# Twenty-four steps of the second block's conditioning moved from the second feed-forward into the first

## The chip, the cores and the metric

The kernel runs on one core of a Trainium2 chip, in one launch. The metric is the device time of one execution in microseconds (us), as the median of three runs.

## The reference, cut to what matters

512 tokens of width 1024 go through two blocks in float32. The first block has three sublayers, each of the form `x + w * gate * norm(fn(norm(x) * (1 + scale) + shift))`: a feed-forward, a mixer and a second feed-forward. The second block has two layers, each a mixer and a mixture of experts. Shift, scale and gate of every sublayer come from a conditioning vector, by one product of a vector with a matrix per block (and per layer in the second block):

```python
def swiglu(h, w_in, w_out):
    g, u = jnp.split(h @ w_in, 2, axis=-1)          # 1024 -> 2 x 2816
    return (jax.nn.silu(g) * u) @ w_out             # 2816 -> 1024
...
ada = (jax.nn.silu(c) @ w_ada[l] + b_ada[l]).reshape(B, N_SUB, 3, D)
...
x = sublayer(x, 0, lambda h: swiglu(h, ffn1_w_in[l], ffn1_w_out[l]), 0.5)
x = sublayer(x, 1, mixer, 1.0)
x = sublayer(x, 2, lambda h: swiglu(h, ffn2_w_in[l], ffn2_w_out[l]), 0.5)
...
def adaln(cond, mod_w, mod_b):                      # second block
    m = jax.nn.silu(cond) @ mod_w + mod_b           # 1024 -> 6 x 1024
    return jnp.split(m, 6, axis=-1)
...
sh1, sc1, g1, sh2, sc2, g2 = [m[:, None, :] for m in adaln(c, mod_w[i], mod_b[i])]
if need_ctx_in:                                     # layer 0 alone
    csh1, csc1, cg1, csh2, csc2, cg2 = adaln(c_ctx, mod_w[i], mod_b[i])
```

The conditioning of the second block depends on nothing that the first block computes, so it may be done at any time before the second block begins.

## The kernel before, in words

**Layout and products.** Activations lie transposed: 1024 channels in eight groups of 128 partitions, 512 tokens along the free side. Every float32 weight chunk (mostly 128 x 1024, 512 KB) is loaded by SyncE into a `raw` buffer (four of them), cast by ScalarE to a high half (L159) and reduced by VectorE to a low half (L160). The halves are called `w` (eleven buffers) or `wk` (in one of 25 general tiles, `k4`). A product is three matmuls: high weight by high activation (L164), high by low (L165), low by high (L166). The split activations are `hh` and `hl`. There are three `aux` buffers (tag `mv`), two psum buffers `pb` (gate and up), three `pa` (outputs) and one `pt` (the norms' sums).

**Conditioning.** `mv_group` (L221) cuts a vector-matrix product into steps. A step loads one 512 KB row block of the matrix into an `aux` buffer (L231) and multiplies it by the vector, held ready in a tile, and sums along the row in one VectorE instruction (L235, a multiply-sum). A row that is needed with two vectors (`s2` from `c`, `s3` from `c_ctx`) gets two multiply-sums, the first with its product in a throw-away `junk` tile. The steps wait in a list, `bgq`; `bg(n)` hands out the next n of them at the place in the program where it is called, `bg_flush` all that are left.

**A feed-forward** (`ffn`, L333) has 22 columns of 128 hidden channels in four parts of 7, 6, 6 and 3. Parts one to three work on all 512 tokens: for each column the gate and up weights are loaded, 48 matmuls go to one `pb`, and then `bg(bg)` hands out steps; for each of eight outputs the down weights are loaded, `bg(bg//3)` hands out steps, and the sums are added to `y` (L440). `bg` is 4 in the first feed-forward and 5 in the second. The fourth part flushes the list, loads three pairs of weights and the down weights (`ka`: high half in `k4`, low half in `aux`), and then goes by halves of 256 tokens: gates of three columns, eight outputs, and a boundary. The boundary is the norm of `y`, the addition to x, the norm of x, and the split into the next stage's `hh` and `hl`: its sums over partitions are matmuls of `pt` (L270), its root is taken at L261 and refined at L262 to L264, and the products, residual steps and scalings are L312, L314 and L300. The first half's boundary is thus meant to run beside the second half's matmuls.

**Order.** Each engine works in order. The order is not that of the text alone: a tile scheduler places each instruction by its priority, which follows the text (pieces in `with self.soon()` are moved ahead), as its operands and buffers come free in a simulated time.

**Around the change.** The list in the first feed-forward holds 56 steps of `w_ada` with the small vector steps behind them, and `pre_mixer1` (rope tables and two small vectors). In the second it holds the Silu of `s2` and `s3`, 96 steps of `mod_w` (16 of them with two vectors), vector steps, and the constants of the mixture of experts. The first feed-forward runs from the start to about 404 us, the mixer from there to 665, the second feed-forward to about 1000.

Of the kernel before, what the change touches and what calls it, by code (L numbers as in the profile page):

```python
# [8 lines left out]
F32 = mybir.dt.float32  # L9
# [4 lines left out]
AF = mybir.ActivationFunctionType  # L14
OP = mybir.AluOpType
# [45 lines left out]
class Prog:  # L61
# [161 lines left out]
    def mv_group(self, arr, g, outs, now=False):  # L223

        def step(m):
            def go():
                if now:
                    w = self.k4(F32, "mv")
                else:
                    w = self.aux()  # L230
                self.nc.sync.dma_start(w, arr[g * 8 + m])  # L231
                for i, (s, dst) in enumerate(outs):
                    last = i == len(outs) - 1
                    junk = w if last else self.k4(F32, "junk")
                    self.nc.vector.scalar_tensor_tensor(  # L235
                        junk, w, 1.0, s, op0=OP.mult, op1=OP.mult, accum_out=dst[:, m:m + 1])
            return go
        for m in range(8):
            if now:
                step(m)()  # L240
            else:
                self.bgq.append(step(m))
# [1329 lines left out]
def program(tc, A, stop=None):  # L1572
    nc = tc.nc
    with ExitStack() as ctx:
        K = Prog(tc, A, ctx)
# [30 lines left out]
        with K.soon():  # L1606
# [8 lines left out]
            r, t = (K.pg() for _ in range(2))  # L1615
# [29 lines left out]
        def post_boundary(j, nxt):  # L1645
            def go(hs, acc, y):
                acc2 = K.postnorm(hs, acc, y, Gp1[j])
                if nxt is not None:
                    nxt(hs, acc2)
            return go  # L1650

        ffw = lambda n: (A[n + "_in"], [A[f"{n}_out{i}"] for i in range(len(FF_PARTS))])
# [6 lines left out]
            K.diff_lambda()  # L1659

        K.queue(pre_mixer1)
        K.ffn(h, *ffw("ffn1"), post_boundary(0, to if stop != "ffn1" else None), bg=4, lead=lead)
        K.bg_flush()
        if stop == "ffn1":
# [11 lines left out]
        to2 = To(G1[2], sh1[2])  # L1676
# [7 lines left out]
        if stop == "mix1":  # L1684
            return finish()


        s2, s3 = K.k4(F32, "s2"), K.k4(F32, "s3")
        for t, i in ((s2, 1), (s3, 2)):
            nc.sync.dma_start(t, A["c_rep"][i])  # L1690

        def silus():
            with tc.issue_after(K.gated):
                for t in (s2, s3):
                    nc.scalar.activation(t, t, AF.Silu)

        K.queue(silus)
        mod = [[K.gvec("mod") for _ in range(6)] for _ in range(2)]
        G2 = [[K.gvec("G2") for _ in range(2)] for _ in range(2)]
        cmod = [K.gvec("cm") for _ in range(2)]  # L1700
        Gc = K.gvec("Gc")

        def mod_vecs(l, i):

            for g in range(3 * i, 3 * i + 3):
                nc.vector.tensor_add(mod[l][g], mod[l][g], K.vec("mod_b", 48 * l + 8 * g, 8))
            gn = K.vec(("n1g", "n2g")[i], 8 * l, 8)
            nc.vector.scalar_tensor_tensor(G2[l][i], mod[l][3 * i + 1], 1.0, gn, op0=OP.add, op1=OP.mult)

        def ctx_vecs():  # L1710
            for g in range(2):
                nc.vector.tensor_add(cmod[g], cmod[g], K.vec("mod_b", 8 * g, 8))
            nc.vector.scalar_tensor_tensor(Gc, cmod[1], 1.0, K.vec("n1g", 0, 8), op0=OP.add, op1=OP.mult)

        for l in range(2):
            for g in range(6):
                outs = [(s2, mod[l][g])]
                if l == 0 and g < 2:
                    outs = [(s3, cmod[g])] + outs
                K.mv_group(A["mod_w"][l], g, outs)  # L1720
                if g == 2 and l == 0:
                    K.queue(ctx_vecs)
                if g % 3 == 2:
                    K.queue(lambda l=l, i=g // 3: mod_vecs(l, i))
        if stop == "ffn2":
            K.bgq = []
            to3 = None
        else:
            to3 = To(G2[0][0], mod[0][0], to2.h)
        K.queue(K.moe_consts)  # L1730
        for l in range(2 if stop != "ffn2" else 0):
            K.queue(lambda l=l: K.moe_shift(l, mod[l][3], mod[l][5]))
        K.ffn(to2.h, *ffw("ffn2"), post_boundary(2, to3), bg=5)
        K.bg_flush()
        if stop == "ffn2":
            return finish()
# [2 lines left out]
        for l in range(2):  # L1739
# [10 lines left out]
            def evac2(m, hs, py, acc):  # L1750
# [5 lines left out]
                nc.vector.scalar_tensor_tensor(xm, py, g1[:, m:m + 1], xm, op0=OP.mult, op1=OP.add)  # L1756
                nc.scalar.activation(open_["xg"][m][:, hs], xm, AF.Copy, scale=G2[l][1][:, m:m + 1])
                K.sq_add(xm, acc, m)
# [40 lines left out]
            routed = K.route(open_["lg"])  # L1799
            to_next = To(G2[1][0], mod[1][0]) if l == 0 and stop != "moe0" else None  # L1800
            open_next = K.moe(l, first, routed, tab, g2, to_next, K.odd_first if to_next else None)
# [176 lines left out]
```

## Time and profile before

| | |
|---|---|
| median of the runs | 1971.92 us (1971.67 to 1973.52, 3 runs) |
| profiled execution | 1968.39 us, span 1966.5 us |
| mean granted clock | 0.971 |
| TensorE busy | 1826.9 us, 93% |
| VectorE busy | 1300.0 us, 66% |
| ScalarE busy | 900.6 us, 46% |
| GpSimd busy | 164.4 us, 8% |

Every duration below is from the one profiled execution. PE is TensorE's matmuls, PEld its weight loads, DVE VectorE, ACT ScalarE, POOL GpSimd, SPq the DMA issues of SyncE. PEclk is the granted clock as a share of full speed, the DMA share the mean busy share of 16 DMA engines. A row of a timeline gives the start, the duration, the instruction and, in brackets, how long the engine was idle before it and what ended that. In a row of windows, (x74) counts the instructions of the engine. Matmuls overlap, so the step from one start to the next says more than a matmul's own duration.

### The profile page before, as it was taken

To read this page: it belongs to the slowest core of one execution; us is meant where nothing else is said; L and a number is where in the kernel's file an instruction comes from. 1 tells how busy PE (TensorE), PEld (TensorE's weight loads), DVE (VectorE), ACT (ScalarE), POOL (GpSimd) and SP (SyncE) were. 2 spreads that over 40 slices of the span, in tenths; PEclk is the share of its full clock that TensorE was granted. 3 is DMA by queue.
4 is the path that set the end of the run, shared out by engine and by line. 5 is a ranking of instruction groups with operands and counts; after the bars stand their busy time and mean duration, and the time that the engine had idled before them with its cause. 6 is when DMAs were issued, how large, how long until landed. Compare 5 with 4: busy or idle time off the path is not lost. (4 is left out here: it accounts for less than half of the span.)

```text
span 1966.5 us, 25708 instructions
## 1 busy us (share of the span) xinstructions
PE 1826.9 (93%) x9669; PEld 1502.5 (76%) x9669; DVE 1300.0 (66%) x2205; ACT 900.6 (46%) x1444; POOL 164.4 (8%) x133
## 2 busy tenths in 40 slices
PE   4999999999987999999999998979999799979996
PEld 3778888986746988868898878967666688967663
DVE  8877434686866689888548776656554654457773
ACT  4422323455657552222336664526665632345551
POOL 0000000000000000000000000004442000014431
PEclk9999999999988999999999999989999899979998
DMA  8888333241113247999533000548997523469993
GB/s 325 300 304 287 105 104 98 86 140 64 60 48 118 76 147 258 319 333 317 204 119 126 20 1 1 193 135 269 305 317 265 186 81 128 172 210 350 342 355 82
DMA packets 109474, 361.30 MB, mean 184 GB/s; under 512 B 19593, under 2 KB 20257, under 8 KB 109345
## 3 DMA queue, kind: packets, MB, share of 16 engines
q1 hardware_dynamic: 92640, 328.09, 47.1%
q0 software_dynamic: 16128, 29.41, 5.7%
q10 hardware_dynamic: 576, 2.10, 0.3%
q8 instruction: 79, 1.29, 0.3%
q14 instruction: 51, 0.41, 0.1%
HBM read 354.25 MB, written 34.62 MB: 198 GB/s over the span
## 5 line engine op out<-in xcount | busy, mean ns | idle before, releaser
L160 DVE TENSOR_TENSOR w<-raw,w 128x1024 fp32r<-128x1024 f32 (+3 forms) x192 | 221.8, 1161 | 168.7 <-issue 74.2
L159 ACT CAST w<-raw 128x1024 fp32r<-128x1024 f32 (+3 forms) x192 | 191.2, 1000 | 298.7 <-PE pa L166 95.8
L164 PE MATMUL pb<-hh,w 128*128 128x512 f32 (+1 forms) x800 | 289.3, 364 | 17.6 <-ACT hh L159 14.3
L165 PE MATMUL pb<-hl,w 128*128 128x512 f32 (+1 forms) x800 | 290.1, 363 | 4.7 <-DVE hl L160 4.7
L166 PE MATMUL pb<-hh,w 128*128 128x512 f32 (+1 forms) x800 | 290.4, 363 | 2.0 <-DVE w L160 1.8
L164 PEld LDWEIGHTS pb<-hh,w 128*128 128x128 f32 x800 | 152.2, 191 | 43.5 <-ACT hh L159 16.0
L165 PEld LDWEIGHTS pb<-hl,w 128*128 128x128 f32 x800 | 152.4, 191 | 29.4 <-DVE hl L160 6.7
L166 PEld LDWEIGHTS pb<-hh,w 128*128 128x128 f32 x800 | 152.4, 191 | 26.5 <-DVE w L160 4.1
L160 DVE TENSOR_TENSOR k<-raw,k 128x1024 fp32r<-128x1024 f32 x101 | 121.6, 1219 | 67.2 <-ACT k L159 57.6
L164 PE MATMUL pa<-hh,w 128*128 128x512 f32 (+1 forms) x392 | 142.5, 367 | 3.3 <-ACT sq L286 2.0
L1477 PE MATMUL pb<-w,a 128*128 128x512 f32 x304 | 137.0, 593 | 2.0 <-ACT a L1466 2.0
L165 PE MATMUL pa<-hl,w 128*128 128x512 f32 (+1 forms) x392 | 135.4, 347 | 0.0
L166 PE MATMUL pa<-hh,w 128*128 128x512 f32 (+1 forms) x392 | 135.1, 346 | 0.0
L164 PE MATMUL pa<-k,w 128*128 128x512 f32 x304 | 126.3, 415 | 0.0
L235 DVE SCALAR_TENSOR_TENSOR aux<-aux,s 128x1024 f32<-128x1024 f32 x96 | 115.7, 1221 | 12.1 <-DMA aux<-in_mod_w 11.5
L165 PE MATMUL pa<-act,w 128*128 128x512 f32 x304 | 118.7, 390 | 2.2 <-DVE act L160 2.1
L166 PE MATMUL pa<-k,w 128*128 128x512 f32 x304 | 119.7, 394 | 0.0
L166 PE MATMUL pa<-act,w 128*128 128x512 f32 x304 | 118.4, 390 | 0.9 <-DVE w L160 0.9
L165 PE MATMUL pa<-k,w 128*128 128x512 f32 x304 | 119.2, 392 | 0.0
L164 PE MATMUL pa<-act,w 128*128 128x512 f32 x304 | 118.4, 390 | 0.3 <-ACT w L159 0.3
L159 ACT CAST k<-raw 128x1024 fp32r<-128x1024 f32 x101 | 105.2, 1048 | 8.8 <-DMA tab<-ht 2.6
L1477 PEld LDWEIGHTS pb<-w,a 128*128 128x128 f32 x304 | 57.2, 189 | 60.4 <-issue 53.2
(445 smaller groups left out, 3962.9 us busy)
## 6 DMA issues: line engine op xcount, KB each, us to landing
aux<-in_mod_w SPq DMA_DIRECT2D x96, 512.0 KB
raw<-in_ffn_in SPq DMA_DIRECT2D x88, 512.0 KB
raw<-in_moe_w SPq DMA_DIRECT2D x86, 512.0 KB
aux<-in_w_ada SPq DMA_DIRECT2D x64, 512.0 KB
w<-in_moe_w SPq DMA_DIRECT2D x64, 512.0 KB
k<-in_moe_w SPq DMA_DIRECT2D x42, 512.0 KB
raw<-in_ffn_out SPq DMA_DIRECT2D x32, 384.0 KB
raw<-in_mix_in SPq DMA_DIRECT2D x20, 512.0 KB
```

The lines of the kernel that those rows point to most:

```text
L159: self.cast = self.nc.scalar.copy(hi, src).ins
L160: return self.nc.vector.tensor_sub(lo, src, hi.bitcast(F32)).ins
L164: mm(p, wh, xh, start=start, stop=False)
L165: mm(p, wh, xl, start=False, stop=False)
L166: mm(p, wl, xh, start=False, stop=stop)
L235: self.nc.vector.scalar_tensor_tensor(junk, w, 1.0, s, op0=OP.mult, op1=OP.mult, accum_out=dst[:, m:m + 1])
L1477: nc.tensor.matmul(py[:, ns], a[:, cs], wt[c][:, ns], start=c == 0, stop=c == 1)
```

## The change

In the first feed-forward the list now begins with a piece that loads `c` and `c_ctx` of the second block into `s2` and `s3` and takes their Silu. Behind `pre_mixer1` it ends with three of the twelve groups of the second block's conditioning: groups 0 to 2 of layer 0, 24 steps, 16 of them with two vectors, 40 multiply-sums in all, and the vector steps that go with them. The second feed-forward's list loads `s2` again and takes its Silu again; it has the other 72 steps, and `bg` there is 3 instead of 5. Since the vectors exist only when their piece has run, `mv_group` now looks them up by name. Line numbers behind L233 are higher by one in the changed kernel.

```diff
@@ mv_group
                 for i, (s, dst) in enumerate(outs):
+                    s = self.cvec[s] if isinstance(s, str) else s
                     last = i == len(outs) - 1
@@ before the first feed-forward
         K.queue(pre_mixer1)
+        cvec = {}
+        def silus(*which):
+            def go():
+                for n, i in which:
+                    cvec[n] = K.k4(F32, n)
+                    nc.sync.dma_start(cvec[n], A["c_rep"][i])
+                with tc.issue_after(K.gated):
+                    for n, _ in which:
+                        nc.scalar.activation(cvec[n], cvec[n], AF.Silu)
+            return go
...
+        def mod_group(l, g):
+            outs = [("s2", mod[l][g])]
+            if l == 0 and g < 2:
+                outs = [("s3", cmod[g])] + outs
+            K.mv_group(A["mod_w"][l], g, outs)
+            if g == 2 and l == 0:
+                K.queue(ctx_vecs)
+            if g % 3 == 2:
+                K.queue(lambda: mod_vecs(l, g // 3))
+        K.cvec = cvec
+        K.bgq.insert(0, silus(("s2", 1), ("s3", 2)))
+        for g in range(3):
+            mod_group(0, g)
         K.ffn(h, *ffw("ffn1"), post_boundary(0, to if stop != "ffn1" else None), bg=4, lead=lead)
@@ before the second feed-forward
-        s2, s3 = K.k4(F32, "s2"), K.k4(F32, "s3")
-        for t, i in ((s2, 1), (s3, 2)):
-            nc.sync.dma_start(t, A["c_rep"][i])
...
-        K.queue(silus)
...
+        K.queue(silus(("s2", 1)))
         for l in range(2):
             for g in range(6):
...
+                if l or g > 2:
+                    mod_group(l, g)
...
-        K.ffn(to2.h, *ffw("ffn2"), post_boundary(2, to3), bg=5)
+        K.ffn(to2.h, *ffw("ffn2"), post_boundary(2, to3), bg=3)
```

The order moves in the first feed-forward's last part. The number in a tile's name counts tiles in the order of their allocation, so it is higher in the change: the third column's psum there is `pb_443` before and `pb_504` now.

**TensorE, from the second to the third column of the last part, first half of the tokens, before:**

```order
L165 MATMUL pb_441_2546<-hl_34_123,w_419_2454 128x256
L166 MATMUL pb_441_2546<-hh_33_122,w_420_2455 128x256
L164 MATMUL pb_443_2600<-hh_27_116,w_422_2460 128x256
L165 MATMUL pb_443_2600<-hl_28_117,w_422_2460 128x256
L166 MATMUL pb_443_2600<-hh_27_116,w_423_2461 128x256
```

and now:

```order
L165 MATMUL pb_502_2682<-hl_34_123,w_480_2590 128x256
L166 MATMUL pb_502_2682<-hh_33_122,w_481_2591 128x256
L164 MATMUL pb_504_2736<-hh_27_116,w_483_2596 128x256
L165 MATMUL pb_504_2736<-hl_28_117,w_483_2596 128x256
L164 MATMUL pb_552_3004<-hh_27_116,w_471_2572 128x256
L165 MATMUL pb_552_3004<-hl_28_117,w_471_2572 128x256
L166 MATMUL pb_552_3004<-hh_27_116,w_472_2573 128x256
```

Two matmuls into the third column, TensorE now goes to `pb_552`, the first column of the second half of the tokens, whose 48 matmuls stand before the rest of the third column.

**VectorE, low halves of the last part's weights, before** (`w_420` and `w_423` are low halves of the second and third column, `wk` and `aux` those of the third column's up weights and the down weights):

```order
L160 TENSOR_TENSOR wk_426_2467<-raw_424_2465,wk_425_2466 128x1024
L160 TENSOR_TENSOR w_420_2455<-raw_418_2453,w_419_2454 128x1024
L440 TENSOR_TENSOR pg_143_771<-pg_143_771,pa_404_2389 128x512
L160 TENSOR_TENSOR aux_432_2476<-raw_430_2474,wk_431_2475 128x1024
L160 TENSOR_TENSOR aux_435_2482<-raw_433_2480,wk_434_2481 128x1024
L440 TENSOR_TENSOR pg_143_771<-pg_143_771,pa_408_2415 128x512
L160 TENSOR_TENSOR w_423_2461<-raw_421_2459,w_422_2460 128x1024
L160 TENSOR_TENSOR aux_438_2488<-raw_436_2486,wk_437_2487 128x1024
```

and now (`w_484` is the third column's low half, `wk_487` that of its up weights):

```order
L236 SCALAR_TENSOR_TENSOR junk_440_2387,cm_67_185<-aux_439_2385,s3_131_620 128x1024
L236 SCALAR_TENSOR_TENSOR aux_445_2416,mod_52_170<-aux_445_2416,s2_130_618 128x1024
L236 SCALAR_TENSOR_TENSOR aux_439_2385,mod_51_169<-aux_439_2385,s2_130_618 128x1024
L236 SCALAR_TENSOR_TENSOR aux_450_2445,mod_52_170<-aux_450_2445,s2_130_618 128x1024
L1690 TENSOR_TENSOR cm_67_185<-cm_67_185,c_7_93 128x8
L1684 TENSOR_TENSOR mod_51_169<-mod_51_169,c_7_93 128x8
L160 TENSOR_TENSOR w_484_2597<-raw_482_2595,w_483_2596 128x1024
L236 SCALAR_TENSOR_TENSOR aux_455_2474,mod_52_170<-aux_455_2474,s2_130_618 128x1024
L1691 SCALAR_TENSOR_TENSOR Gc_68_186<-cm_67_185,c_7_93 128x8
L1686 SCALAR_TENSOR_TENSOR G2_62_180<-mod_51_169,c_7_93 128x8
L160 TENSOR_TENSOR wk_487_2603<-raw_485_2601,wk_486_2602 128x1024
L236 SCALAR_TENSOR_TENSOR aux_460_2503,mod_52_170<-aux_460_2503,s2_130_618 128x1024
```

Where low halves followed each other, multiply-sums of the conditioning (L236, `mod` and `cm`) now stand between them.

**TensorE, end of the first feed-forward and start of the mixer, before** (`pa_511` is the last output, `pa_565` and `pb_567` are the mixer's first products):

```order
L164 MATMUL pa_511_3127<-act_429_2473,wk_437_2487 128x256
L165 MATMUL pa_511_3127<-act_429_2473,wk_437_2487 128x256
L166 MATMUL pa_511_3127<-act_429_2473,aux_438_2488 128x256
L164 MATMUL pa_565_3290<-hh_27_116,w_542_3243 128x256
L164 MATMUL pb_567_3342<-w_548_3255,hh_27_116 128x512
L165 MATMUL pb_567_3342<-w_549_3256,hh_27_116 128x512
```

and now (`pa_572` is the last output, `pa_626` and `pb_628` the mixer's first products):

```order
L164 MATMUL pa_572_3263<-act_490_2609,wk_498_2623 128x256
L165 MATMUL pa_572_3263<-act_490_2609,wk_498_2623 128x256
L166 MATMUL pa_572_3263<-act_490_2609,aux_499_2624 128x256
L270 MATMUL pt_541_2956<-acc_525_2909,c_5_89 128x256
L270 MATMUL pt_574_3277<-acc_558_3166,c_5_89 128x256
L164 MATMUL pa_626_3426<-hh_27_116,w_603_3379 128x256
L164 MATMUL pb_628_3478<-w_609_3391,hh_27_116 128x512
L165 MATMUL pb_628_3478<-w_610_3392,hh_27_116 128x512
```

`pt_541` is the first half's second norm, of x; its counterpart before stood 59 matmuls ahead of the last output's end, and now it stands behind it, together with the second half's first norm, `pt_574`.

## Rows read from the trace of the kernel before

**Rows 1.** The forty slices of the page: TensorE's busy tenths and the DMA digits.

```profile
...
PE   4999999999987999999999998979999799979996
...
DMA  8888333241113247999533000548997523469993
...
```

**Rows 2.** Second feed-forward: us; busy PE, PEld, DVE, ACT, POOL; PEclk, DMA, GB/s.

```profile
840.00:860.00 20.00, 17.71 (x74) 13.42 (x74) 17.22 (x27) 5.26 (x7) 0.00 (x0) 1.00 0.89 311
860.00:880.00 20.00, 17.90 (x72) 12.79 (x72) 18.57 (x31) 5.47 (x8) 0.00 (x0) 1.00 0.93 330
```

**Rows 3.** Waits of TensorE, 640 to 1010 us: total us, times, longest us.

```profile
...
PE pb L166 <- DVE w L160: 1.8, 4, 0.5
PE pb L164 <- ACT w L159: 1.3, 2, 1.1
...
```

**Rows 4.** Timeline of TensorE, last part's start and mixer's start: start us, us, instruction.

```profile
...
349.85 0.28 PE L164 MATMUL pb<-hh,w 128*128 128x256 f32 x1
349.97 0.28 PE L165 MATMUL pb<-hl,w 128*128 128x256 f32 x1
...
403.58 0.39 PE L164 MATMUL pa<-hh,w 128*128 128x256 f32 x1 [0.15 <-ACT hh L159]
```

**Rows 5.** Windows of 50 us in the first feed-forward, columns as in rows 2.

```profile
100.00:150.00 50.00, 47.92 (x212) 39.36 (x211) 36.86 (x60) 14.60 (x21) 0.00 (x0) 1.00 0.86 305
300.00:350.00 50.00, 50.00 (x223) 41.43 (x222) 21.29 (x27) 17.93 (x22) 0.00 (x0) 1.00 0.37 115
```

**Rows 6.** Timelines of SyncE's queue (issues) and of ScalarE, 345 to 353 us.

```profile
345.22 0.33 SPq L149 DMA_DIRECT2D raw<-in_ffn_out  x1
...
347.00 0.33 SPq L149 DMA_DIRECT2D raw<-in_ffn_out  x1
...
349.76 1.05 ACT L159 CAST wk<-raw 128x1024 fp32r<-128x1024 f32 x1 [1.79 <-DMA raw<-in_ffn_out]
351.70 1.06 ACT L159 CAST wk<-raw 128x1024 fp32r<-128x1024 f32 x1 [0.89 <-DMA raw<-in_ffn_out]
```

**Rows 7.** Timeline of VectorE in the second feed-forward, two multiply-sums end to end.

```profile
717.20 1.22 DVE L235 SCALAR_TENSOR_TENSOR aux<-aux,s 128x1024 f32<-128x1024 f32 x1
...
718.35 1.22 DVE L235 SCALAR_TENSOR_TENSOR junk<-aux,s 128x1024 f32<-128x1024 f32 x1
```

**Rows 8.** Timeline of VectorE before the last part of the first feed-forward.

```profile
345.75 1.23 DVE L160 TENSOR_TENSOR w<-raw,w 128x1024 fp32r<-128x1024 f32 x1 [0.56 <-PE pa L165]
346.89 0.68 DVE L440 TENSOR_TENSOR pg<-pg,pa 128x512 f32<-128x512 f32 x1
```

**Rows 9.** Timelines of ScalarE and VectorE: the norms' steps, 377 to 404 us.

```profile
377.11 0.42 ACT L286 ACTIVATE sq<-pg 128x256 f32<-128x256 f32 x1 [0.88 <-DVE pg L395]
377.55 1.28 ACT L261 ACT_TABLE_LOAD   x1
378.84 0.47 ACT L261 ACTIVATE hf<-pt,c 128x256 f32<-128x256 f32 x1
...
381.32 0.42 DVE L263 SCALAR_TENSOR_TENSOR hf<-hf,hf 128x256 f32<-128x256 f32 x1
...
382.24 0.76 DVE L312 TENSOR_TENSOR hf<-pg,hf 128x256 f32<-128x256 f32 x2
382.92 0.88 DVE L314 SCALAR_TENSOR_TENSOR x<-hf,ad,x 128x256 f32<-128x256 f32 x2
...
402.16 1.08 ACT L300 ACTIVATE hf<-hf,ad,ad 128x256 f32<-128x256 f32 x2
403.14 0.70 ACT L159 CAST hh<-hf 128x256 fp32r<-128x256 f32 x2
```

**Rows 10.** Windows of 5 us, TensorE alone: us, PE busy, PEclk, DMA share, GB/s.

```profile
660.00:665.00 5.00, 3.00 (x26) 0.99 0.10 7
665.00:670.00 5.00, 5.00 (x29) 0.66 0.83 291
610.00:615.00 5.00, 4.15 (x24) 0.63 0.49 111
```

More of the change, by code (lines that the diff above doesn't have):

```diff
@@ L1661, in program, with mod_vecs, ctx_vecs @@
         K.queue(pre_mixer1)
+        cvec = {}
[8 more added lines that the diff above has]
+            return go
+        mod = [[K.gvec("mod") for _ in range(6)] for _ in range(2)]
+        G2 = [[K.gvec("G2") for _ in range(2)] for _ in range(2)]
+        cmod = [K.gvec("cm") for _ in range(2)]
+        Gc = K.gvec("Gc")
+        def mod_vecs(l, i):
+            for g in range(3 * i, 3 * i + 3):
+                nc.vector.tensor_add(mod[l][g], mod[l][g], K.vec("mod_b", 48 * l + 8 * g, 8))
+            gn = K.vec(("n1g", "n2g")[i], 8 * l, 8)
+            nc.vector.scalar_tensor_tensor(G2[l][i], mod[l][3 * i + 1], 1.0, gn, op0=OP.add, op1=OP.mult)
+        def ctx_vecs():
+            for g in range(2):
+                nc.vector.tensor_add(cmod[g], cmod[g], K.vec("mod_b", 8 * g, 8))
+            nc.vector.scalar_tensor_tensor(Gc, cmod[1], 1.0, K.vec("n1g", 0, 8), op0=OP.add, op1=OP.mult)
+        def mod_group(l, g):
[11 more added lines that the diff above has]
+            mod_group(0, g)
         K.ffn(h, *ffw("ffn1"), post_boundary(0, to if stop != "ffn1" else None), bg=4, lead=lead)
@@ L1685, in program @@
             return finish()
-        s2, s3 = K.k4(F32, "s2"), K.k4(F32, "s3")
-        for t, i in ((s2, 1), (s3, 2)):
-            nc.sync.dma_start(t, A["c_rep"][i])
[L1692 to L1695, printed above, removed]
-        K.queue(silus)
[L1698 to L1713, printed above, removed]
+        K.queue(silus(("s2", 1)))
         for l in range(2):
             for g in range(6):
[L1717 to L1724, printed above, removed]
+                if l or g > 2:
+                    mod_group(l, g)
         if stop == "ffn2":
```

## The prediction

> **What bounds the kernel now.** Three views were read in this order: the forty slices, the windows of the two feed-forwards, and the timelines around the end of the first one. The slices [rows 1] show TensorE at nine tenths or more in most of the first seven and from the fifteenth to the twenty-second; the DMA digits are 8 early in the first feed-forward, then 2 to 3, and up to 9 in the second. So the loads that the change moves leave a stretch with full DMA engines for one with idle ones. The 20 us windows [rows 2] show all that there is to win: TensorE is idle 2.29 and 2.10 us in the two worst windows of the second feed-forward, at a DMA share of 0.89 and 0.93, and 0.1 us in the rest of 700 to 1000 us. The waits name late weights, low halves and casts [rows 3]. This is 4.4 us of 1968: TensorE, not DMA, sets the length of both feed-forwards.
>
> The end of the first feed-forward has no slack to give. Its last part begins at 349.85 us, 256-column matmuls follow each other every 0.12 us, and the first matmul of the mixer starts at 403.58 after a wait of 0.15 us [rows 4]: the norm chain of the first half of the tokens ends just as TensorE runs out of other work.
>
> **The change part by part.**
>
> *Two Silus and two 512 KB loads at the head of the queue.* They run at about 100 us, where TensorE is busy 47.92 of 50 us and ScalarE 14.60 [rows 5]. ScalarE's two steps are as large as a cast of 1.05 us [rows 6], and weights are loaded some ten us ahead. I take 0; without that cover it would be the two loads at the 305 GB/s of that window, 3.4 us.
>
> *Twenty-four steps of conditioning, 40 multiply-sums, into the first feed-forward.* One takes VectorE 1.15 us from start to start [rows 7], 46 us in all. VectorE is busy 21 of 50 us before the end of this feed-forward, TensorE 50.00 [rows 5], so the amount is covered. The place is not. The steps stand behind the old queue and behind the rope tables, and are given out in part three only. In the order of the change 20 of the 40 stand on VectorE between the low half of the second up weight (`w_481`) and the release of the third pair's psum (`pb_504`). VectorE works in order: while it waits for `w_481`, whose buffer TensorE frees, loaded rows pile up behind it, and then they are in front of what TensorE needs.
>
> The walk: before, that low half starts at 345.75 and takes 1.14 [rows 8], so it ends at 346.9. I begin at 348.0, 1.1 later, since the last activation of part three has multiply-sums ahead of it too. Up to the psum release stand 20 multiply-sums (22.9), two additions at 0.6 [rows 8], three gate products at 0.34 (as long as the products of [rows 9]), two low halves at 1.14 and four small steps of 0.15: 28.0, so 376.0 us if every row has landed. But there are three row buffers, and a load is issued only when an earlier multiply-sum frees one. A 512 KB load issued at 345.22 was waited for until 349.76, and one of 347.00 until 351.70: 4.5 and 4.7 us in a quiet stretch [rows 6]. With 4.6 us for each, four of the later rows are late (by 0.6, 0.6, 1.5 and 0.9 us) and the release comes at about 379.8. I take this, the measured landing; 376.0 is the lower bound. By the Trainium skill (DMA: Bandwidth & Descriptors, "Anatomy of one DMA — SWDGE (gpsimd) path") a transfer takes about 2.0 us plus its bytes at 436 GB/s (told there of GpSimd's path, while SyncE issues the loads here), an estimate of 3.2 us; by it few rows would be late and the release would stand near 376. The rows above say 4.6.
>
> In place of the late pair, TensorE's order takes 48 gate matmuls of the second half of the tokens first, and later 39 more. They fill the wait, but are then gone as cover: before, 218 matmuls of the second half's work stood between the first half's last product and the mixer, now 130.
>
> From the psum release on, 241 matmuls at 0.12 us (28.9) lead to the last product of this feed-forward, and three short waits (0.9 for the matmul of the first norm, whose sum stands behind a mixer weight that VectorE splits, 0.6 for the last activation, 0.2 for a psum buffer): 410.4 us. If TensorE never waited it would be 402.1 (349.85, 432 matmuls, one norm matmul of 0.4).
>
> *What follows on that last product.* In the new order the second norm of the first half comes directly behind it; before it stood 59 matmuls ahead. VectorE's list ends with the addition of that product (0.42), one residual step (0.40), two products (0.68), a sum (0.34) and two more residual steps (0.79): 2.6. ScalarE squares the last piece (0.33), has six more squares queued (1.9), loads a table (1.28) and takes the root (0.47): 4.0. Then VectorE's three steps at 0.46, one product at 0.34, ScalarE's two scalings (1.0) and a cast (0.4): 3.1. Together 9.8 us [rows 9]. So the mixer begins at 410.4 + 9.8 = 420.2, against 403.58: **+16.6 us**. It cannot be less than 402.1 + 9.8 = 411.9, +8.3; were each of the last rounds of loads 1.5 us later still, about +22.
>
> *The clock after that wait.* TensorE stands nearly still for some ten us. In this profile a wait of 2 us (660 to 665) is followed by 5 us at a granted clock of 0.66, and 610 to 615, behind 5 us without a matmul, shows 0.63 [rows 10]; with two levels, 2.4 and 1.2 GHz, 0.66 over 5 us is 1.7 us of lost time. I take **+1.7**; 0 if the mixer's first products are fed too slowly to use the full clock, 5 if it stays low for ten us.
>
> *The second feed-forward without those rows.* Beside a 512 KB weight chunk the queue now has two rows where it had three: 1.57 MB in the 5.4 us of a chunk, 290 GB/s, where three ask for 390 and the window of [rows 2] got 330. The late weights go: **-4.3 us** of the 4.4; bounds 0 and -4.5. Its last part keeps its order, with the full 218 matmuls of cover. Nothing behind the second feed-forward is moved.
>
> **Sum.** +16.6 + 1.7 - 4.3 = +14.0 us, of the profiled 1968.4: 1982.4. The profiled execution is 3.5 us below the median of the runs, 1971.9, which I compare with: **1986 us**. From the bounds: 8.3 + 0 - 4.5 = +3.8 to 22 + 5 + 0 = +27.
>
> **The rivals.** A measurement of this kernel tells about 0.2% from no change, that is 3.9 us.
> - *No row is late.* The release at 376.0, the last product at 404.9, the mixer at 414.7: +11.1, and with clock and relief +8.5, 1980 us. For it: DMA at a share of 0.37 in that stretch [rows 5]. Against it: the two landings of [rows 6] were measured in just such a stretch. It is the outcome that the 3.2 us of the Trainium skill's page would bring. 0.15.
> - *No relief in the second feed-forward.* All its rows are now loaded before part three, none spread into it, so the early parts may stay as full as they were: +18.3, 1990 us. 0.15.
> - *Longer rounds and a clock that stays low:* +24 or more, 1996 us. Against it: the DMA engines are idle there. 0.10.
> - *The boundary gives back.* The second half's norm is ready earlier relative to the mixer's start, since its matmul no longer waits between projections; if that pays 4 us in the mixer and the walk is at its floor, 1972 us. Against it: TensorE is at 0.15 us of idle behind 403 as it is. 0.07.
> - *Faster:* the relief of 4.3 decides, because the early gate matmuls of the second half cover the wait and the chain behind the last product is short. It holds if the mixer begins at or before 404, and gives 1967.5 us. For it: before, this chain ended 0.4 us behind the last product. Against it: then the second norm stood 59 matmuls ahead; now its nine to ten us are in the order itself. 0.06.
> - *The change does not do what it says* holds for "spread thinner" only, and is the second rival.
>
> **The numbers.** The forecast has 0.47 (its own range 1982 to 1990). The range reaches from the rival without late rows, and 4 us below for a chain that is partly shorter, to the long rounds: 1975 to 1995. Left out are the faster and the equal case and part of the long one, about 0.18. Slower by over 0.2%: 0.47 + 0.15 + 0.15 + 0.10 = 0.87; equal 0.07; faster 0.06.
>
> **What would show it.** Right: the first matmul of the mixer (`pa<-hh`) near 420 us with a wait of some 9 us on ScalarE's `hh` and the norm's sums; multiply-sums end to end on VectorE from 348 to 380; TensorE waiting there for the low half `wk` or a psum buffer; a granted clock below 1 just behind the mixer's start; no idle windows at 140 us into the second feed-forward. Wrong: a first mixer matmul before 408, or TensorE idle of 4 us left in the second feed-forward. The most exposed step is the 3.8 us of late rows; the firmest is the 9.8 behind the last product.

## The result, and the profile after

The changed kernel takes **1990.96 us** (median of 6 runs, 1989.11 to 2002.31) against 1971.85 us before (6 runs): 19.1 us more, ratio 1.0108 with a 95% interval of 1.0091 to 1.0124. (The ratios here and below are as recorded; they are not the quotients of the medians, which is 1.0097 here.) It is slower, inside the range that was given, 5 us above the forecast of 1986. The profiled execution took 1993.17 us (span 1990.9), 2.2 above its median, where that of before lay 3.5 below.

The slices of the changed kernel, TensorE and DMA, to be read beside [rows 1]:

```profile
PE   4999999889986999999999998979999699979996
...
DMA  8888426631112249884241200537998523559993
```

TensorE's eighth and ninth digit (348 to 448 us) fell from 9 to 8; the DMA digits of the seventh and eighth slice rose from 3 and 2 to 6, and in the second feed-forward they reach 9 as before, only for a shorter time.

**Ahead of the mixer.** TensorE's waits between 340 and 430 us in the changed kernel (before, there was one of 0.2):

```profile
PE pt L270 <- DVE acc L289: 7.0, 2, 3.8
PE pb L164 <- DVE pg L363: 5.7, 2, 4.1
PE pa L164 <- ACT hh L159: 1.4, 1, 1.4
PE pb L166 <- DVE w L160: 0.6, 1, 0.6
PE pa L164 <- ACT act L159: 0.3, 1, 0.3
```

The same waits in TensorE's timeline, with the mixer's first matmul as the last row:

```profile
380.32 0.58 PE L164 MATMUL pb<-hh,w 128*128 128x256 f32 x1 [4.07 <-DVE pg L363]
...
417.02 1.22 PE L270 MATMUL pt<-acc,c 128*128 128x256 f32 x2 [3.80 <-DVE acc L289]
421.44 1.22 PE L270 MATMUL pt<-acc,c 128*128 128x256 f32 x2 [3.20 <-DVE acc L289]
424.11 0.58 PE L164 MATMUL pa<-hh,w 128*128 128x256 f32 x1 [1.45 <-ACT hh L159]
```

VectorE's timeline at the first of these: the last late row, and behind it the gate product that frees the psum:

```profile
347.40 1.22 DVE L236 SCALAR_TENSOR_TENSOR junk<-aux,s 128x1024 f32<-128x1024 f32 x1
...
378.70 1.23 DVE L236 SCALAR_TENSOR_TENSOR aux<-aux,s 128x1024 f32<-128x1024 f32 x1 [3.12 <-DMA aux<-in_mod_w]
...
379.85 0.75 DVE L363 TENSOR_TENSOR pg<-pg,pb 128x256 f32<-128x256 f32 x2
```

Behind both stretches of waiting the granted clock is low. TensorE alone in 5 us windows (us, busy, granted clock, DMA share, GB/s):

```profile
375.00:380.00 5.00, 1.25 (x11) 0.87 0.93 351
380.00:385.00 5.00, 4.68 (x22) 0.50 0.48 173
...
415.00:420.00 5.00, 1.22 (x2) 0.62 0.00 0
420.00:425.00 5.00, 2.11 (x5) 0.50 0.00 0
425.00:430.00 5.00, 5.00 (x19) 0.51 0.00 0
```

The mixer begins 20.5 us late (424.11 against 403.58). At the matmul that ends the mixer, the one with a wait of 2.0 us for a square, the delay is 20.0 us (683.92 against 663.91). The mean granted clock between these two points is 0.96, and 0.95 before.

**In the second feed-forward** the small weight waits of [rows 3] are mostly gone, and larger ones stand in their place, at the first output of the first and of the second part:

```profile
786.81 0.50 PE L164 MATMUL pa<-act,w 128*128 128x512 f32 x1 [1.61 <-ACT act L159]
788.90 0.80 PE L165 MATMUL pa<-act,w 128*128 128x512 f32 x1 [1.59 <-DVE act L160]
...
898.11 0.79 PE L164 MATMUL pa<-act,w 128*128 128x512 f32 x1 [3.55 <-ACT act L159]
```

VectorE shows why: the last column's gate product (785.43) stands behind rows that it waits for.

```profile
780.93 1.23 DVE L236 SCALAR_TENSOR_TENSOR aux<-aux,s 128x1024 f32<-128x1024 f32 x1 [0.40 <-DMA aux<-in_mod_w]
783.27 1.23 DVE L236 SCALAR_TENSOR_TENSOR aux<-aux,s 128x1024 f32<-128x1024 f32 x1 [1.11 <-DMA aux<-in_mod_w]
784.42 1.08 DVE L160 TENSOR_TENSOR w<-raw,w 128x896 fp32r<-128x896 f32 x1
785.43 0.68 DVE L363 TENSOR_TENSOR pg<-pg,pb 128x512 f32<-128x512 f32 x1
```

Windows of 20 us, TensorE alone, from 100 and from 200 us behind the mixer's end:

```profile
783.92:803.92 20.00, 16.80 (x60) 0.83 0.81 274
...
883.92:903.92 20.00, 16.45 (x60) 0.84 0.91 317
903.92:923.92 20.00, 20.00 (x88) 0.99 0.34 113
```

Idle 3.20 and 3.55 us, and a granted clock of 0.83 and 0.84 on top. From 903.92 on the DMA share is 0.34: all 72 rows have been loaded by then. They were not spread: ahead of the last gate products of parts one, two and three 26, 46 and 0 rows are multiplied, where it was 18, 50 and 28 before. The first two parts have 72 rows instead of 68. From the matmul at the mixer's end to the first norm of the first half of the tokens, this feed-forward takes 374.4 us (683.92 to 1058.32) against 370.2 before (663.91 to 1034.11; it does not end at about 1000 us, but runs on behind that).

### The profile page after: what moved, and what is told of

It reads as the page before. It is cut to its first block, busy times and chain, and to the rows that moved or that the text cites. A ratio compares the mean times of both kernels' runs of the same rounds, so it can differ in the third digit from the quotient of the medians.

```text
span 1990.9 us, 25683 instructions
## 1 busy us (share of the span) xinstructions
PE 1831.6 (92%) x9669; PEld 1509.5 (76%) x9669; DVE 1299.6 (65%) x2205; ACT 900.8 (45%) x1445; POOL 162.9 (8%) x133
## 5 line engine op out<-in xcount | busy, mean ns | idle before, releaser
L236 DVE SCALAR_TENSOR_TENSOR aux<-aux,s 128x1024 f32<-128x1024 f32 x96 | 116.5, 1222 | 32.3 <-DMA aux<-in_mod_w 30.9
L164 PE MATMUL pa<-act,w 128*128 128x512 f32 x304 | 120.7, 398 | 5.2 <-ACT act L159 5.2
L165 PE MATMUL pa<-act,w 128*128 128x512 f32 x304 | 121.1, 398 | 3.6 <-DVE act L160 3.6
L166 PE MATMUL pa<-act,w 128*128 128x512 f32 x304 | 120.4, 396 | 0.0
L362 ACT ACTIVATE pg<-pb 128x512 f32<-128x512 f32 (+1 forms) x52 | 27.5, 532 | 166.7 <-PE pb L166 166.7
```

The source lines that it names most:

```text
L164: mm(p, wh, xh, start=start, stop=False)
L165: mm(p, wh, xl, start=False, stop=False)
L166: mm(p, wl, xh, start=False, stop=stop)
L236: self.nc.vector.scalar_tensor_tensor(junk, w, 1.0, s, op0=OP.mult, op1=OP.mult, accum_out=dst[:, m:m + 1])
L362: self.gated = nc.scalar.activation(sv, pg[:, :n], AF.Silu).ins
```

## The experiments

Twelve kernels; each is compared with the kernel before on the same chip, where that has a median of 1972.26 to 1973.66 us. Two lengths are read from each trace: when the mixer begins, and the second feed-forward's stretch just defined. How many multiply-sums stand on VectorE ahead of each gate product says where the steps went; in the tables a bar ends a part, and the last group is the fourth part's first half.

```
first feed-forward     part two          part three         fourth
before                 21 5 5 1 0 0   |  0 0 0 0 0 0     |  0
change                 21 5 5 3 0 0   |  0 0 0 1 6 7     |  12 4 8
f1_5                   21 5 5 3 0 0   |  0 0 7 8 7 10    |  8
j_aux, j_aux_p2        21 5 5 6 4 6   |  22 5 0 0 0 0    |  0
jp53                   13 4 5 4 5 5   |  12 5 5 6 4 6    |  14
jp43                   11 4 3 4 3 4   |  12 3 4 3 6 5    |  20 2 3
jmix53                 14 6 6 6 6 6   |  21 5 5 4 5 3    |  1

second feed-forward    part one    part two          part three        fourth
before                 6 6 8 7 7 | 24 5 5 6 4 6   |  18 5 5 0 0 0   |  0
change, no24, j_aux    6 5 6 6 3 | 20 6 4 6 5 5   |  0 0 0 0 0 0    |  0
b_f2_3                 4 7 6 8 8 | 20 4 4 6 5 5   |  18 5 5 5 2 0   |  0
b4p2                   6 6 8 8 7 | 14 4 4 4 3 4   |  12 4 4 3 4 4   |  13
p2, jp53, jp43         2 6 3 3 3 | 10 3 3 3 3 3   |  10 3 3 3 3 3   |  5
```

Part one of the second feed-forward shows the five columns after the first two. The first number of a part also counts what stands among the eight outputs ahead of it.

### no24: the moved steps left out

```diff
-        for g in range(3):
-            mod_group(0, g)
+        for t in (*mod[0][:3], *cmod):
+            nc.vector.memset(t, 0.0)
+        K.queue(ctx_vecs)
+        K.queue(lambda: mod_vecs(0, 0))
```

> The changed kernel without its 24 moved steps: they are computed nowhere (their vectors start at zero); the Silus at the head of the first list stay, and the second feed-forward has its 72 steps with bg=3. Theory: the whole loss ahead of the mixer comes from these 24 steps at the end of the first list, and the second feed-forward lost time by itself, since the 72 steps are not spread there but stand in front of the last gate products of its first two parts. Then the mixer begins at 403 to 405 us as before, TensorE waits 3 us at the end of each of the first two parts of the second feed-forward, and the time is 1976 us (before plus 4; 1974 to 1978). Rival 1, the relief is there and the profile of the change was an unlucky execution: 1967.5 us, no wait over 1 us between 690 and 1000 us. Rival 2, the Silus and their loads at the head cost part of the 20 us: the mixer begins after 408 us and the time is 1981 us or more.

Measured: 1972.37 us against 1972.26, ratio 1.0000 (0.9985 to 1.0016). Its timeline of TensorE:

```profile
402.73 0.39 PE L164 MATMUL pa<-hh,w 128*128 128x256 f32 x1
...
769.23 0.79 PE L164 MATMUL pa<-act,w 128*128 128x512 f32 x1 [4.76 <-ACT act L159]
...
878.79 0.51 PE L164 MATMUL pa<-act,w 128*128 128x512 f32 x1 [3.48 <-ACT act L159]
```

So the moved steps, and they alone, cost the change about 18.6 us (1990.96 less 1972.37). Both rivals are out. The second feed-forward with a quarter of its rows gone gains nothing: 374.8 us, with the waits at the ends of the parts. The time missed the expected 1976: the 4 us had been taken from two profiled executions, and that of before was a quick one.

### f1_5: the same steps earlier

```diff
-        K.ffn(h, ..., bg=4, lead=lead)
+        K.ffn(h, ..., bg=5, lead=lead)
```

> The changed kernel with bg=5 instead of 4 in the first feed-forward, so that the same 24 steps are handed out before its last part. Theory (place): only steps that stand among the last part's low halves and gate products hurt; the second norm of the first half stands 59 matmuls ahead of the last product again, the mixer begins at 404 to 409 us, and with the second feed-forward as in the change the time is 1976 us (1974 to 1981). Rival (amount): 46 us of multiply-sums and 12.6 MB of rows more in this feed-forward cost the same wherever they stand: the mixer begins at 418 us or later and the time is 1988 us or more.

Measured: 1987.68 us, ratio 1.0085 (1.0068 to 1.0101); the mixer begins at 416.89. The theory fell: TensorE's order in the last part is back, and two thirds of the delay are still there; the figures lie just short of the rival's. TensorE now waits in the third part:

```profile
314.06 0.79 PE L166 MATMUL pb<-hh,w 128*128 128x512 f32 x1 [3.02 <-DVE w L160]
324.90 0.49 PE L164 MATMUL pa<-act,w 128*128 128x512 f32 x1 [2.85 <-ACT w L159]
328.88 0.79 PE L166 MATMUL pa<-act,w 128*128 128x512 f32 x1 [3.49 <-DVE w L160]
```

and VectorE, in windows of 10 us of the whole core, is busy without a pause there while TensorE is not:

```profile
310.00:320.00 10.00, 6.98 (x19) 5.22 (x18) 10.00 (x17) 0.62 (x1) 0.00 (x0) 0.66 0.57 197
```

### silu_head: the two Silus alone

```diff
+        def early():
+            tt = [K.k4(F32, "e2"), K.k4(F32, "e3")]
+            for t, i in zip(tt, (1, 2)):
+                nc.sync.dma_start(t, A["c_rep"][i])
+            with tc.issue_after(K.gated):
+                for t in tt:
+                    nc.scalar.activation(t, t, AF.Silu)
+        K.bgq.insert(0, early)
```

> The kernel before with the change's first piece alone: two 512 KB loads and two Silus at the head of the first list, whose results nothing uses; all 96 steps stay in the second feed-forward. Theory: 0, hidden at 100 us, 1972 us (1970 to 1974), the mixer begins at 403 to 404 us. Rival, the loads are on the path there: 3.4 us or more, 1975 us and up.

Measured: 1973.69 us, ratio 1.0015 (1.0000 to 1.0029), mixer at 404.11. The trace shows no loss. The interval alone leaves up to 5.7 us open; no24, which has the same piece, showed no loss either.

### b_f2_3: the smaller bg alone

```diff
-        K.ffn(to2.h, ..., post_boundary(2, to3), bg=5)
+        K.ffn(to2.h, ..., post_boundary(2, to3), bg=3)
```

> The kernel before with bg=3 instead of 5 in the second feed-forward, all 96 steps there. Theory: bg says where steps stand in the text, not when they run, and the order of VectorE's steps is nearly the same; the loss of the change there comes from the missing second multiply-sums, which leave VectorE nothing to do but wait for rows. Then 1972 us (1970 to 1975). Rival, the smaller bg itself puts the rows in front of the last gate products: waits of 3 us at the ends of parts one and two and 1976 us or more. Rival, bg spreads the rows and gives the relief of 4.3 us: 1968 us.

Measured: **1966.28 us**, ratio 0.9973 (0.9963 to 0.9983); the second feed-forward takes 364.6 us. The theory fell, and the second rival held: with all 96 steps, bg=3 carries rows into the third part (18 5 5 5 2) and the waits for weights go; 2.9 us of waiting for activations remain at the first output of part two. What the change got wrong is therefore not bg alone. The first two parts take 77 multiply-sums here; the change has 72 for this feed-forward, so the same bg left its third part empty.

### j_aux: the junk tile elsewhere

```diff
-                    junk = w if last else self.k4(F32, "junk")
+                    junk = w if last else self.aux(s="junk")
```

> The changed kernel with one word altered: the throw-away product of a row's first multiply-sum goes to an aux buffer and not to one of the 25 k4 tiles. Theory: the moved steps run so late because their junk tile waits for a free k4 tile, and those are taken by activations and the rope tables until the third part of the first feed-forward is nearly done; with the tile elsewhere the 40 multiply-sums stand in the second and third part, the last part keeps its old order, the mixer begins at 402 to 406 us against 424, and the time is that of the kernel without these steps, 1972 us (1970 to 1977). Rival (amount): 46 us more of VectorE's work cost wherever they stand, as bg=5 showed: the mixer begins at 412 us or later and the time is 1982 us or more.

Measured: 1983.18 us, ratio 1.0063 (1.0044 to 1.0082); the mixer begins at 413.17. The first half of the theory is shown: with the junk tile out of k4 the steps begin six columns earlier in the order, so it was the wait for a k4 tile that pushed them into the last part. The second half fell, and the rival's figures were met, though not for its reason (see jp53). The steps now stand ahead of the last gate product of part two, and TensorE waits there:

```profile
228.70 0.80 PE L164 MATMUL pa<-act,w 128*128 128x512 f32 x1 [5.67 <-ACT act L159]
```

### p2: multiply-sums behind the gate product, second feed-forward only

```diff
-                    nc.vector.tensor_mul(sv, sv, pu[:, :n])
+                    self.gprod = nc.vector.tensor_mul(sv, sv, pu[:, :n]).ins
...
+                    with self.tc.issue_after(self.gprod) if self.behind else nullcontext():
                         self.nc.vector.scalar_tensor_tensor(
```

`issue_after` adds no wait on the chip: it fixes the order on VectorE.

> The changed kernel with one addition for the second feed-forward alone: a multiply-sum stands on VectorE behind the gate product of the column ahead of it in the text, so that three run per column. Theory: the changed kernel got no relief there because the scheduler moves all 72 steps into the first two parts (five to six rows per column), and late rows hold up the last gate products; spread over all three parts they don't. The mixer begins at 424 us as in the change, TensorE waits under 2 us between 700 and 1000 us (7 us in the change), the second feed-forward is 9 us shorter, and the time is 1982 us (1980 to 1985). Rival: the waits at the ends of the parts come from the weights' own loads and remain; 1988 us or more.

Measured: 1975.53 us, ratio 1.0016 (1.0003 to 1.0030), 15.4 us under the change and better than the range. The stretch is 360.8 us (682.00 to 1042.84), without a wait over 1 us behind its first gates. TensorE alone in 20 us windows: the first gates, with their wait of 2.1 us, and then the places where the change stood still:

```profile
702.00:722.00 20.00, 17.91 (x131) 1.00 0.07 20
...
782.00:802.00 20.00, 20.00 (x90) 1.00 0.88 304
...
882.00:902.00 20.00, 20.00 (x90) 1.00 0.75 260
902.00:922.00 20.00, 20.00 (x90) 1.00 0.69 241
```

It gained 13.6 us and not 9 because the clock no longer falls behind the waits: 6.75 us of waits, and 20 x 0.17 + 20 x 0.16 = 6.6 of clock. The mixer begins at 420.28 in this execution, 3.8 us sooner than in the change's, though TensorE, VectorE and ScalarE have the same order up to there in both kernels. This second execution of the same order is used below.

### j_aux_p2: both edits

> Both edits together. Theory: they act in different stages and add up: mixer at 402 to 406 us, second feed-forward without waits of over 1 us, 1963 us (1960 to 1968), under the kernel before. Rival (amount, or waits that remain): 1972 us or more.

Measured: 1967.06 us, ratio 0.9979 (0.9968 to 0.9989). Faster than before and within the range, but by luck: the mixer still begins at 413.38, 7 us behind the theory, and the stretch of 360.8, 13.6 us under the change's where p2 was expected to gain 9, makes up for part of it.

### b4p2: the kernel before, only spread

The edit of p2 in the kernel before, with bg=4 in the second feed-forward.

> The kernel before with all 96 steps in the second feed-forward, bg=4, and multiply-sums behind the gate product of the column ahead. Theory: spreading alone gives the relief, without moving a step into the first feed-forward: 1965 us (1962 to 1969). Rival: 96 steps are too many to be spread over three parts, the rest runs into the last part (thirteen multiply-sums ahead of its first gate product) and holds it up as the moved steps did in the first feed-forward: 1975 us or more.

Measured: **1961.91 us**, ratio 0.9953 (0.9935 to 0.9971); just under the range; the stretch is 361.8 us. Spreading alone gives more than the whole relief that the change was to bring. The thirteen multiply-sums ahead of the last part's first gate product cost nothing that the trace shows.

### one: one multiply-sum per moved row

```diff
-                outs = [("s3", cmod[g])] + outs
+                outs = outs
```

(The context's two vectors are set to zero at the start.)

> The changed kernel without the 16 multiply-sums with s3 (the context's two vectors are left out, they start at zero): the same 24 rows are loaded in the first feed-forward, each multiplied once, and no junk tile is needed. Theory: what costs is VectorE being full where doubled rows stand close together; with one multiply-sum per row it is not, so the mixer begins at 402 to 405 us though all 12.6 MB are loaded there, and the time is 1972 us (1969 to 1975), as without any of these steps. Rival (the rows' loads cost): the mixer begins at 408 us or later and the time is 1978 us or more.

Measured: 1983.99 us, ratio 1.0056 (1.0035 to 1.0078), mixer at 412.51. The theory fell: with 24 multiply-sums instead of 40, and in the place that j_aux has, the wait is the same:

```profile
228.83 0.79 PE L164 MATMUL pa<-act,w 128*128 128x512 f32 x1 [5.66 <-ACT act L159]
```

Doubled rows are not what costs. Whether the loads do is told by the next run.

### jp53: spread in both feed-forwards

The edit of j_aux, that of p2 without its condition, and bg=5 in the first, 3 in the second feed-forward.

> The changed kernel with junk in an aux buffer, bg=5 in the first and 3 in the second feed-forward, and in both a multiply-sum stands behind the gate product of the column ahead of it. Theory: 80 steps with 96 multiply-sums spread over three parts (4 to 6 per column) fill VectorE nowhere ahead of a gate product; fourteen that run into the last part stand ahead of its first gate product, which has no other cover, and may cost up to 6 us. The mixer begins at 403 to 410 us, the second feed-forward takes 361 us as in the run with both edits, and the time is 1958 to 1964 us. Rival (amount): the mixer begins at 413 us or later and the time is 1967 us or more.

Measured: **1956.31 us**, ratio **0.9905** (0.9890 to 0.9920). It beats both kernels, by 17.4 and about 35 us. The first matmul of the mixer, and the one at its end:

```profile
399.88 0.38 PE L164 MATMUL pa<-hh,w 128*128 128x256 f32 x1
...
659.59 0.39 PE L164 MATMUL pa<-hh,w 128*128 128x256 f32 x1 [2.00 <-ACT sq L288]
```

All 24 rows, all 40 multiply-sums and 12.6 MB are in the first feed-forward, which ends 3.7 us earlier than before. That is better than the range, since the fourteen multiply-sums ahead of the last part cost nothing. The spread of the 56 old steps could have hidden a cost of the amount, but no idle time is left in which it could lie; TensorE alone from 100 us to the mixer:

```profile
100.00:399.88 299.88, 299.61 (x1523) 1.00 0.69 234
```

In the kernel before it is idle 2.4 us there (100 to 403.58). The amount costs nothing; the rival of amount is out.

### jmix53: the moved steps mixed among the old ones

jp53, with the moved steps put one by one between the last 40 pieces of the old list.

> As the run before (junk in aux, bg=5 and 3, multiply-sums behind the gate product ahead), and the 24 moved steps are mixed one by one among the last 40 old steps of the first list, so that none is left for the last part. Theory: with 3 to 6 multiply-sums per column and one ahead of the last part's first gate product nothing is held up: the mixer begins at 402 to 405 us, and the time is 1958 us (1956 to 1962), the least of all. Rival (amount): the doubled rows fill VectorE at the end of the second part, where 21 stand among eight outputs, the mixer begins at 408 us or later and the time is 1965 us or more.

Measured: 1962.94 us, ratio 0.9947 (0.9931 to 0.9964), mixer at 405.93, with waits of 1.32 and 1.42 us at the ends of parts two and three. Just outside the range, the mixer 0.9 us later than expected, and worse than jp53, which has fourteen multiply-sums ahead of the fourth part's first gate product where this has one. The theory's worry about those fourteen was wrong; why the mixed list waits at the ends of the parts is left open.

### jp43: spread, but too late

jp53 with bg=4 in the first feed-forward.

> As jp53 with bg=4 in the first feed-forward: 20 multiply-sums stand ahead of the last part's first gate product and seven more among its others, and the second norm of the first half stands 17 matmuls ahead of the last product (59 in the kernel before, behind it in the change). Theory: the last part is held up by about what VectorE must do first, 20 x 1.15 less the cover of the third part's last products, and the norm's chain of about 10 us is covered by 17 matmuls (2 us) only: the mixer begins at 412 to 422 us, the time is 1968 to 1976 us. Rival, only the norm's place behind the last product costs: the mixer begins at 404 to 408 us, and the time is 1958 to 1962 us.

Measured: 1962.89 us, ratio 0.9937 (0.9918 to 0.9956), mixer at 411.53. The waits are of the expected kind, and the mixer's start lies just below the expected 412:

```profile
368.68 0.39 PE L166 MATMUL pa<-act,aux 128*128 128x256 f32 x1 [2.02 <-DVE aux L160]
374.30 0.62 PE L164 MATMUL pa<-act,wk 128*128 128x256 f32 x3 [1.76 <-ACT act L159]
410.87 1.22 PE L271 MATMUL pt<-acc,c 128*128 128x256 f32 x2 [4.20 <-DVE acc L290]
```

The 4.2 us stand ahead of the second half's first norm, which TensorE does before the mixer. The first half's second norm ran at 404.05, 17 matmuls ahead of the last product, and its chain came to ScalarE's cast into `hh` only at 410.51. Why the median is 5 us below the range is open: the second feed-forward is the short one (360.8), but it is in jp53 too.

## Why the prediction was right, step by step

**The place of the steps: right; the size of the delay was in part luck.** The first multiply-sum after the second up weight's low half started at 347.40 (walk: 348.0), five rows were late by 4.7 us in all (0.63, 0.26, 0.30, 0.36 and 3.12; walk: four, 3.6 and 3.8 in the sum), and the gate product that frees the psum ran at 379.85 (walk: 379.8). The sum agrees, its terms less so: four rows were late by 1.6 us only, and the last one took 6.6 us to land (issued at 372.03, landed at 378.60), where the walk has 4.6. The DMA engines were not idle either: their share is 0.81, 0.80 and 0.93 in the three windows of 5 us from 365 us on, against the 0.37 of [rows 5].

The same order ran a second time, in p2 (L238 there is the multiply-sum, L365 the gate product):

```profile
349.62 1.22 DVE L238 SCALAR_TENSOR_TENSOR junk<-aux,s 128x1024 f32<-128x1024 f32 x1
...
371.75 1.23 DVE L238 SCALAR_TENSOR_TENSOR aux<-aux,s 128x1024 f32<-128x1024 f32 x1 [0.56 <-DMA aux<-in_mod_w]
...
377.68 0.75 DVE L365 TENSOR_TENSOR pg<-pg,pb 128x256 f32<-128x256 f32 x2
...
378.15 0.39 PE L165 MATMUL pb<-hh,w 128*128 128x256 f32 x1 [0.93 <-DVE pg L365]
...
420.28 0.58 PE L165 MATMUL pa<-hh,w 128*128 128x256 f32 x1 [1.45 <-ACT hh L160]
```

One row was late there, by 0.56, and the gate product ran at 377.68: 28.1 us behind the first multiply-sum, the walk's 28.0 without late rows, where the change's execution took 32.5. So VectorE's work ahead of the gate product is shown by both, and the late rows are a matter of the single execution, 0.6 to 4.7 us. p2's is the outcome of the first rival, "no row is late". The recorded landings of the rows issued between 350 and 374 us are 3.3 to 6.6 us (median 4.4) in the change and 3.4 to 4.2 (median 3.5) in p2; the 4.6 of [rows 6] belong to weights. An estimate of 3.2 us, worked out from a figure that the Trainium skill (DMA: Bandwidth & Descriptors, "Anatomy of one DMA — SWDGE (gpsimd) path") gives for GpSimd's path, lies near p2's median and below that of the change.

**The last product: right, 2.8 us short.** Forecast 410.4; measured 413.2 (417.02 less the wait of 3.80). The step that was left out: behind the wait for the psum the clock is low as well. It was 0.50 in the 5 us behind it, 2.5 us, where the prediction charged the clock for the second wait alone. In p2, with a wait of 0.93 us, the clock stayed at 1.00, and the last product ended at 409.4 (413.20 less 3.81).

**What follows on the last product: right, 1.1 us short.** 10.9 us in both executions (413.2 to 424.11 and 409.4 to 420.28) against 9.8. At the mixer's start the delay is 20.5 in the change's execution and 16.7 in p2's; the forecast was 16.6.

**The clock behind it: seen, but not in the sum.** 0.51 in the first 5 us of the mixer is 2.4 us; forecast 1.7. At the mixer's end the delay is 20.0, no more than at its start, and the mean granted clock of the whole mixer is as before. The term adds nothing.

**The relief: wrong.** The step "beside a 512 KB weight chunk the queue now has two rows where it had three" did not hold, nor did the -4.3 us, and the prediction's own sign against it, 4 us of idle time left in the second feed-forward, was there. The first two parts got 72 rows where they had 68; that all rows stand ahead of part three is told by the second rival, and the sum did not use it. The rows ran at five to six per column and were done by 903 us, with a DMA share of 0.8 to 0.9 until then. The late weights did go, but VectorE ran out of work, waited for rows, and held the last gate product of each part. no24 puts the whole effect on the second feed-forward at 0.1 us, with an interval of about 3 to each side: the second rival, at 1990 us, was the right one for this stage. (The stretch is 4.2 us longer than before's; silu_head, which has the old second feed-forward, takes 371.5.)

That the relief itself exists is shown by b_f2_3, p2 and b4p2, whose stretch is 5.6 to 9.4 us shorter than before's. It is larger than the idle 4.4 us of [rows 2], for TensorE's busy time in the stretch falls too, from 363.5 us to 358.3 in b4p2. A low clock does not explain that, since silu_head has 362.7 at 1.00; the cause is open.

**The sum.** Up to the mixer's end 18.3 us were forecast (16.6 and 1.7) and 20.0 measured; for the second feed-forward -4.3 forecast, about 0 by the medians. That is 20 in place of 14.0, and the medians differ by 19.1. The time lies in the range because the place, the large term, was right; the missing relief is most of what is left.

**The reason behind the place** was not in the prediction: a doubled row's junk tile waits for one of the 25 k4 tiles (j_aux). And the place in the last part is only one of several that cost: f1_5, j_aux and one lost 9 to 13 us at the mixer's start at other gate products and low halves.

What stays open: what sets the pace at which the scheduler places the steps in the second feed-forward. Where they are not tied, the first two parts take 84 multiply-sums (before), 77 (b_f2_3) or all 72 that there are (change, no24).

## What to carry to other kernels

Background work on an engine that works in order costs by what stands behind it, not by its amount: 46 us of it cost 19 us where they stood ahead of low halves and gate products, and nothing in jp53, where each batch was tied behind the last urgent step and handed out early enough. The tie alone does not do it: jp43 has the same ties and hands out one step less per turn, 27 multiply-sums were left for the last part, and the mixer began 8 us late. A count handed out per loop turn does not set the pace if a scheduler is free to move the work; fix the order against the urgent instruction, and see in the order of each engine where a moved step ended up, and which pool its scratch tile comes from.

A wait of 3 to 4 us on TensorE should be charged with the lower clock behind it, in the change's execution 2.5 to 3.4 us more each time in the two feed-forwards; whether it is still there at the end of the next stage must be looked up, as the mixer shows. And a walk that meets the measured moment is not yet right: a second execution of the same order tells which of its terms belong to the order.

## What the runs showed of the hardware that was not expected

The clock's fall behind short waits: after 4.07 us of waiting the granted clock was 0.50 for 5 us, the lower of the two levels, 1.2 GHz; after 3.55 us it was 0.84 over 20 us; around the wait of 2.1 us at the first gates of p2 it stayed at 1.00, while 2.0 us of waiting in [rows 10] were followed by 0.66. In the profile of before the two windows of 20 us behind the mixer's end stand at 0.91, where the change, p2 and jp53 have 1.00. Such differences between executions of one kernel fit the spread of its runs, 1965 to 1979 us: 4 us between two profiled executions say little.

The landing of a 512 KB load: in the same stretch of the same order, one execution's rows landed in 3.4 to 4.2 us and another's in 3.3 to 6.6, at a DMA share of 0.8 and more in both towards its end.
